# The cross-attention output projection computed with seven block products in place of eight

## The chip, the cores and the metric

The kernel runs on one core of one Trainium2 chip. The metric is the device time of one execution in microseconds (us). Before the change the median of three runs is 860.67 us (860.36 to 862.97).

The engines are called as the profile calls them: PE multiplies matrices (PEld loads its weights beside that), DVE and ACT work on vectors, POOL is used here for small vector operations and for issuing transfers, and SP issues transfers. Each engine carries out its own instructions in order and waits for the others by semaphores.

## The reference

One layer of a hybrid encoder on a sequence of 512 tokens with 1024 features, all in float32:

```
x = x + token_mixer(rmsnorm(x))
x = x + cross_attention(rmsnorm(x), rmsnorm(mem))     # 4 heads of 256, 256 memory tokens
x = x + relu(rmsnorm(x) @ w_up)**2 @ w_down           # 4096 hidden features
y = rmsnorm(x)

def cross_attention(xn, memn):
    q, (k, v) = heads(xn @ w_q), heads(split(memn @ w_kv))
    p = softmax(q @ k.T / 16)
    return concat_heads(p @ v) @ w_o                  # (512 x 1024) @ (1024 x 1024)
```

The change concerns the last line, the product with `w_o`, called `xo` in the kernel.

## The kernel before

**Precision.** Every float32 product is made as three PE products of fp32r parts: each operand is split into hi and lo, and `mm3` (L235 to L238) issues hi by hi, hi by lo and lo by hi. Splitting is `split_out` (L231 to L233): ACT copies the source into hi, DVE subtracts hi from the source into lo.

**Weights.** All weights lie in one packed array of blocks of 128 x 1024 (512 KB). SP streams them in the order of the list `SEQ` into the `st` buffers (three of them), each is split into one of three `wh` and one of three `wl` buffers, and PE takes these in turn. `weights` runs three blocks ahead.

**Cross-attention.** For each head h, `proj_d("xq", ...)` makes the queries, and `xattn_chain(h)` then runs in three pieces: scores and softmax; transposes of the softmax and their split into the buffer `pT` (of the two `as` buffers); the product with the values, whose result for half j of the head is split into a tile of `os_` (128 features by 512 tokens, hi and lo). The chains run inside the projections: `tick` and `drain` emit the next piece. The order on PE in this part is a scheduler's, not written by hand; from the MLP on it is the order of the code.

**The output projection.** `proj_res("xo", 0, os_, ...)` goes over two column halves c. In each, `proj_t` takes four weight blocks q (two 128-feature tiles k each) and four token tiles t: 4 x 4 x 2 matmul triples, 192 matmuls of 128x512 in both halves. The blocks for heads 0 to 2 run first, `drain` finishes head 3, and the fourth block follows. Each finished token tile is added to the residual `xr` (L822, DVE), its squares are summed (`stats`, L816, ACT), and `transp` (L830 on PE, L835 on ACT, L836 on DVE) transposes it into `x3T`, the operand of the MLP.

**The MLP.** It is done for four groups f of 1024 hidden features. `proj_d("up", ...)` makes 128 hidden features at a time; the norm's factor per token, a pow on POOL (L917), is transposed into a row by `rms_row` (L923) after the first block. The down product of a group is a 2 x 2 block product made with seven block products, P1 to P7, instead of eight. Four of them take sums of the blocks of the activations, made by DVE (L1033 to L1036) and split again; four take sums of weight blocks: T2 of three blocks for P6, U of two for P5, T3 of two for P7, and T2 with a fourth block for P4. These sums are made by the DMA: `sum_loads` (L951 in `add_block`) has POOL issue one plain transfer and then accumulating ones into the same place, in two column groups g. T2 and U lie in the two `as` buffers, T3 in two `gate` buffers. Products are gathered in three pairs of PSUM banks, and each is added into the residual or subtracted from it when it ends.

For the first group the sums T2, U and T3 are asked for ahead of the first up projection, behind the cross-attention in the code; they start as soon as their buffers are free.

Of the kernel before, what the change touches and what calls it, by code (L numbers as in the profile page):

```python
# [11 lines left out]
F32R = mybir.dt.float32r  # L12
# [6 lines left out]
P = 128  # L19
# [26 lines left out]
def _split_order():  # L46
    def d(m, c0, n):
        return [("d", m, 0, c0 + P * i) for i in range(n)]

    def t(m, k0, c0, n=4):  # L50
        return [("t", m, k0 + 2 * i, c0) for i in range(n)]

    seq = t("in", 0, 1536) + [("d", "gate", 0, 0)]
    for g in (0, 512, 1024, 2048):
        seq += d("in", g, 2)
    for g in (0, 512, 1024):
        seq += d("in", g + 256, 2)
# [12 lines left out]
    seq += [("t", "down", 8 * f + 2 * g, 512) for f in range(4) for g in range(2)]  # L70
    return seq


SEQ = _split_order()
SIDX = {key: i for i, key in enumerate(SEQ)}
NSTREAM = len(SEQ) - 8


@with_exitstack
def trunk(ctx: ExitStack, tc: tile.TileContext, x, mem, wpk, vec, cst, lmask, rmask, rows, out):  # L80
# [165 lines left out]
            o.append((t[:, b:b + n], t[:, b + n:b + 2 * n]))  # L246
        return o

    def proj_d(mat, c0, xs, n=512, count=2):

        for j in range(count):
            wh, wl = weights(("d", mat, 0, c0 + P * j))
            ps = mmb()
            for k in range(8):
                z = slice(k * P, k * P + P)
                mm3(ps[:, :n], wh[:, z], wl[:, z], xs[k][0], xs[k][1], k == 0, k == 7)
                if k == 3:
                    tick()
            yield ps
            tick()  # L260
# [540 lines left out]
    xr = {}  # L801
# [98 lines left out]
            split_out(d[:, 0:512], d[:, 512:1024], ps)  # L900
            os_[2 * h + j] = hl(d)

    for h in range(4):
        qd[h] = []
        for ps in proj_d("xq", 256 * h, x2):
            d = YT1()
            split_out(d[:, 0:512], d[:, 512:1024], ps)
            qd[h].append(d)
        chains.append(xattn_chain(h))

    st2 = misc[:, 34:42]
    x3T = XT()
    proj_res("xo", 0, os_, (x3T, V_MLP), st2, drain)
    x3 = xk(x3T)
    ms2 = rstd_tok(st2)
    r4 = tiny(4)
    gp.tensor_tensor(out=r4, in0=ms2, in1=nh.to_broadcast([P, 4]), op=ALU.pow)  # L917
    rrow = RG()

    def rms_row():  # L920
        ps = smb()
        for t in range(4):
            pe.transpose(ps[:, t * P:t * P + P], r4[:, t:t + 1].to_broadcast([P, P]), ident)  # L923
        sc.activation(rrow[:, 0:512], ps, AF.Copy)

    ORDER = ("P1", "P2", "P6", "P5", "P7", "P3", "P4")
    JOBS = [("P1", 0), ("P2", 0), ("P1", 1), ("P2", 1)] + [(p, g) for p in ORDER[2:] for g in range(2)]  # L930
    jobs_hl, sums = {}, {}

    def block(f, g, kh, c):
        return SIDX["t", "down", 8 * f + 2 * g + 4 * kh, 512 * c]

    def sum_loads(f, names):

        parts = {"T2": ((0, 1), (1, 1), (0, 0)), "U": ((0, 1), (0, 0)), "T3": ((0, 1), (1, 1))}
        for nme in names:
            t = A16() if nme != "T3" else None  # L940
            for g in range(2):
                sums[f, nme, g] = G4()[:, :] if t is None else t[:, g * 1024:g * 1024 + 1024]
# [12 lines left out]

    def job(f, n):

        if n >= len(JOBS):
            if f < 3:
                split(SIDX["d", "up", 0, 1024 * (f + 1)] + n - len(JOBS))  # L960
            return None
        p, g = JOBS[n]
        if p in PLAIN:
            i = block(f, g, *PLAIN[p])
            split(i)
# [1 line left out]
        if (f, n) not in jobs_hl:  # L967
# [4 lines left out]
            if p == "P6":  # L972
                add_block(s_, block(f, g, 1, 0))
        return jobs_hl[f, n]

    def finish(t, r, first):

# [10 lines left out]
    def add_to(t, c, ps, sign, fin=False):  # L988
# [13 lines left out]
        gp.tensor_tensor(out=r, in0=s1, in1=nh, op=ALU.pow)  # L1002
        finish(t, r, pieces[t])

    ctx.enter_context(tc.manual_schedule(engines={mybir.EngineType.PE}))
    for f in range(4):

# [2 lines left out]
        for p in range(4):  # L1010
            a = []
            for j in range(2):
                ps, = proj_d("up", 1024 * f + P * (p + 4 * j), x3, count=1)
                if f == 0 and p == 0 and j == 0:
                    rms_row()
                y = T2()[:, 0:512]
                v.scalar_tensor_tensor(out=y, in0=ps, scalar=0.0, in1=rrow[:, 0:512], op0=ALU.max, op1=ALU.mult)  # L1017
                sc.activation(y, y, AF.Square)
                a.append(y)
# [10 lines left out]
            sa, sb_ = T2()[:, 0:512], T2()[:, 0:512]  # L1030
            s1, s2, s3, s4 = sa[:, 0:256], sa[:, 256:512], sb_[:, 0:256], sb_[:, 256:512]
            x1, x2_, x3_, x4 = a[0][:, 0:256], a[0][:, 256:512], a[1][:, 0:256], a[1][:, 256:512]
            v.tensor_tensor(out=s1, in0=x2_, in1=x4, op=ALU.subtract)  # L1033
            v.tensor_tensor(out=s2, in0=s1, in1=x1, op=ALU.subtract)  # L1034
            v.tensor_tensor(out=s3, in0=x1, in1=x2_, op=ALU.subtract)
            v.tensor_tensor(out=s4, in0=x3_, in1=s2, op=ALU.add)  # L1036
            ya, yb = YT1(), YT1()
            split_out(ya[:, 0:512], ya[:, 512:1024], sa)
            split_out(yb[:, 0:512], yb[:, 512:1024], sb_)
            e["P5"], e["P6"] = [(ya[:, u:u + 256], ya[:, 512 + u:768 + u]) for u in (0, 256)]  # L1040
            e["P7"], e["P3"] = [(yb[:, u:u + 256], yb[:, 512 + u:768 + u]) for u in (0, 256)]
# [5 lines left out]
        X, Y, Z = [smb(), smb()], [mmb(), mmb()], [smb(), smb()]  # L1047
        bank = {"P1": X, "P2": Y, "P5": Z, "P6": X, "P3": Z, "P7": X, "P4": X}
        into = {"P1": (0, 0, 1), "P2": (0, 0, 1), "P5": (2, 1, 1), "P6": (0, 1, -1), "P3": (0, 1, 1), "P7": (2, 1, -1), "P4": (2, 0, 1)}
        last = {"P2", "P3", "P7", "P4"}  # L1050

        def product(p, g, u, w, first, end):
            for k in range(2):
                ah, al = [t[:, u * P:u * P + P] for t in sta[2 * g + k][p]]
                bh, bl = [t[:, k * 512:k * 512 + 512] for t in w]
                new = first and k == 0 and p in ("P1", "P2", "P5")
                fl = dict(skip_group_check=True)
                ps = bank[p][u]
                pe.matmul(ps, lhsT=ah, rhs=bh, start=new, stop=False, **fl)  # L1059
                pe.matmul(ps, lhsT=ah, rhs=bl, start=False, stop=False, **fl)  # L1060
                pe.matmul(ps, lhsT=al, rhs=bh, start=False, stop=end and k == 1, **fl)  # L1061

        def ahead(n):
            with tc.high_priority():
                for m in range(n, n + 3):
                    job(f, m)
                i = max(hl_tiles)
                for m in range(i + 1, i + 4):
                    load(m)
            if n == 8 and f < 3:  # L1070
                sum_loads(f + 1, ("U", "T3"))
            return job(f, n)

        def done(p, u):
            t0, c, sign = into[p]
            add_to(t0 + u, c, bank[p][u], sign, fin and p in last)

        n = 0
        while n < len(JOBS):
            p, g = JOBS[n]  # L1080
            if p == "P4":
                ws = [ahead(n), ahead(n + 1)]
                for u in range(2):
                    for g in range(2):
                        product(p, g, u, ws[g], False, g == 1)
                    done(p, u)
                n += 2
                continue
            w = ahead(n)
            for u in range(2):  # L1090
                product(p, g, u, w, g == 0, g == 1)
                if g == 1:
                    done(p, u)
            n += 1


# [88 lines left out]
```

## Time and profile before

| | |
|---|---|
| median of the runs | 860.67 us |
| the profiled execution | 861.91 us |
| its span, from the first instruction to the last | 860.1 us |
| mean granted clock of PE | 0.995 |
| matmul instructions of PE in the trace | 4438 |
| weight blocks loaded by SP | 133 of 512 KB, 3.3 us to landing in the median |
| weight blocks loaded by POOL into `as` | 48 of 512 KB, 7.2 us |
| weight blocks loaded by POOL into `gate` | 16 of 512 KB, 7.1 us |

In rows of the profile, `mm<-wh,yT` stands for the output and the operands by the names of the tiles, and `[3.01 <-PE mm L238]` for the idle time ahead of an instruction and what ended it. In this stage `yT` are the head outputs and `x3T` appears as `xT`. The output projection stands at 467.7 to 521 us of the span, with the last pieces of head 3 in it, and the first up projection follows.

### The profile page before, as it was taken

Reading aid. Unit: us, or ns where it says so; the run is one execution under the profiler, and the core shown is the slowest. Engines: PE = TensorE matmul, PEld = TensorE weight load, DVE = VectorE, ACT = ScalarE, POOL = GpSimd, SP = SyncE. Lnnn points to the kernel's source line nnn. Section 1 sums busy time; section 2 is a strip of 40 time slices with the busy share of each in tenths; the row PEclk is TensorE's granted clock in tenths of the full one; section 3 lists DMA queues with packets and bytes.
Section 4 is the critical chain, followed back from the end, with each engine's and each line's share of the span. In section 5 each row is a group of like instructions: output and inputs, shape, how many; then the busy total and the mean of one; then the engine's idle time right before and its main releaser. Section 6 shows DMA issues by size and latency. Waiting matters only on the chain.

```text
span 860.1 us, 11677 instructions
## 1 busy us (share of the span) xinstructions
PE 840.4 (98%) x4438; PEld 693.8 (81%) x4438; DVE 566.6 (66%) x996; ACT 423.7 (49%) x773; POOL 67.4 (8%) x114
## 2 busy tenths in 40 slices
PE   7999999998999999999999999999999999999995
PEld 5888788887987987888888887888888888888884
DVE  5558874599347987654545446676667656856675
ACT  5336454445558576454443346553454344434544
POOL 1000000100010000100001200003101210220001
PEclk9999999999999999999999999999999999999998
DMA  7332223122152232452213852348935993698322
GB/s 265 123 119 75 73 80 136 46 94 76 50 147 74 99 123 99 158 135 98 74 50 110 206 149 76 97 130 229 282 118 127 275 259 99 173 284 203 123 50 98
DMA packets 32682, 113.62 MB, mean 132 GB/s; under 512 B 3761, under 2 KB 3889, under 8 KB 32626
## 3 DMA queue, kind: packets, MB, share of 16 engines
q1 hardware_dynamic: 23120, 78.84, 26.9%
q0 software_dynamic: 9216, 33.56, 17.7%
q8 instruction: 35, 0.57, 0.3%
q10 hardware_dynamic: 290, 0.47, 0.2%
q14 instruction: 21, 0.17, 0.1%
HBM read 110.76 MB, written 2.10 MB: 131 GB/s over the span
## 4 chain that ended last, share of the span: by engine, by line
PE 85%; issue 6%; DVE 5%; DMA 1%; ACT 1%; POOL 1%; POOLq 0%; ACTq 0%; DVEq 0%
PE mm L236 19%; PE mm L237 19%; PE mm L238 18%; PE sm L1059 5%; PE sm L1060 5%; PE sm L1061 5%; PE sm L688 2%; PE sm L673 2%; PE sm L454 2%; DVE wl L233 1%; PE sm L384 1%; PE mm L1060 1%; PE mm L1061 1%; PE mm L1059 1%; DVE a L479 1%
## 5 line engine op out<-in xcount | busy, mean ns | idle before, releaser
L232 ACT ACTIVATE wh<-st 128x1024 fp32r<-128x1024 f32 x133 | 141.1, 1061 | 223.2 <-PE mm L237 118.8
L233 DVE TENSOR_TENSOR wl<-st,wh 128x1024 fp32r<-128x1024 f32 x133 | 162.7, 1223 | 106.8 <-ACT wh L232 101.7
L236 PE MATMUL mm<-xT,wh 128*128 128x512 f32 x544 | 216.0, 398 | 0.0
L237 PE MATMUL mm<-xT,wh 128*128 128x512 f32 x544 | 213.2, 392 | 0.4 <-DVE xT L836 0.4
L238 PE MATMUL mm<-xT,wl 128*128 128x512 f32 x544 | 212.3, 390 | 0.0
L237 PEld LDWEIGHTS mm<-xT,wh 128*128 128x128 f32 x544 | 102.2, 188 | 22.9 <-DVE xT L836 2.0
L236 PEld LDWEIGHTS mm<-xT,wh 128*128 128x128 f32 x544 | 102.2, 188 | 22.2 <-issue 0.7
L238 PEld LDWEIGHTS mm<-xT,wl 128*128 128x128 f32 x544 | 102.1, 188 | 21.3 <-issue 0.2
L951 POOL DMA_DIRECT2D as<-in_wpk x48 | 36.5, 770 | 312.0 <-DVE wl L233 187.2
L1017 DVE SCALAR_TENSOR_TENSOR t<-mm,rg 128x512 f32<-128x512 f32 x32 | 22.1, 691 | 55.1 <-PE mm L238 55.0
L236 PE MATMUL mm<-wh,yT 128*128 128x512 f32 x128 | 50.6, 395 | 0.0
L238 PE MATMUL mm<-wh,yT 128*128 128x512 f32 x128 | 50.4, 394 | 0.0
L237 PE MATMUL mm<-wl,yT 128*128 128x512 f32 x128 | 50.4, 393 | 0.0
L1059 PE MATMUL sm<-wh,yT 128*128 128x512 f32 x128 | 49.8, 389 | 0.0
L1060 PE MATMUL sm<-wl,yT 128*128 128x512 f32 x128 | 49.8, 389 | 0.0
L1061 PE MATMUL sm<-wh,yT 128*128 128x512 f32 x128 | 49.8, 389 | 0.0
L232 ACT ACTIVATE wh<-as 128x1024 fp32r<-128x1024 f32 x24 | 25.5, 1062 | 33.3 <-PE sm L1061 23.7
L233 DVE TENSOR_TENSOR wl<-as,wh 128x1024 fp32r<-128x1024 f32 x24 | 29.4, 1226 | 13.7 <-ACT wh L232 13.7
L174 POOL TENSOR_TENSOR tiny<-tiny,misc 128x4 f32<-128x4 f32 (+1 forms) x14 | 11.9, 850 | 282.5 <-DVE tiny L172 282.5
L990 DVE TENSOR_TENSOR vv<-vv,sm 128x512 f32<-128x512 f32 x48 | 31.0, 680 | 1.2 <-PE sm L1061 1.2
L236 PEld LDWEIGHTS mm<-wh,yT 128*128 128x128 f32 x128 | 24.1, 188 | 5.3 <-DVE a L233 0.5
L232 ACT ACTIVATE yT<-t 128x512 fp32r<-128x512 f32 x32 | 19.8, 630 | 17.0 <-DVE t L1034 16.5
(275 smaller groups left out, 1510.5 us busy)
## 6 DMA issues: line engine op xcount, KB each, us to landing
st<-in_wpk SPq DMA_DIRECT2D x133, 512.0 KB, 3.3
as<-in_wpk POOLq DMA_DIRECT2D x48, 512.0 KB, 7.2
gate<-in_wpk POOLq DMA_DIRECT2D x16, 512.0 KB, 7.1
as<-in_x SPq DMA_DIRECT2D x4, 512.0 KB, 6.3
vv<-in_x SPq DMA_DIRECT2D x8, 256.0 KB, 4.2
out<-vv SPq DMA_DIRECT2D x7, 256.0 KB, 2.3
a<-in_mem SPq DMA_DIRECT2D x2, 512.0 KB, 5.1
t<-in_rows SPq DMA_DIRECT2D x2, 256.0 KB, 6.1
```

What stands on the lines that cost most here:

```text
L232: sc.activation(dst_hi, src, AF.Copy)
L233: v.tensor_tensor(out=dst_lo, in0=src, in1=dst_hi.bitcast(F32), op=ALU.subtract)
L236: pe.matmul(ps, lhsT=ah, rhs=bh, start=first, stop=False)
L237: pe.matmul(ps, lhsT=ah, rhs=bl, start=False, stop=False)
L238: pe.matmul(ps, lhsT=al, rhs=bh, start=False, stop=last)
L454: pe.matmul(ps[:, t * P:t * P + P], lhsT=A[j][:, s * 512 + t * P:s * 512 + t * P + P], rhs=vh[s][:, h * P:h * P + P], start=(s == 0), stop ...
L951: gp.dma_start(out=dst, in_=wpk[idx], **kw)
L990: v.tensor_tensor(out=z, in0=z, in1=ps, op=ALU.add if sign > 0 else ALU.subtract)
L1017: v.scalar_tensor_tensor(out=y, in0=ps, scalar=0.0, in1=rrow[:, 0:512], op0=ALU.max, op1=ALU.mult)
L1059: pe.matmul(ps, lhsT=ah, rhs=bh, start=new, stop=False, **fl)
L1060: pe.matmul(ps, lhsT=ah, rhs=bl, start=False, stop=False, **fl)
L1061: pe.matmul(ps, lhsT=al, rhs=bh, start=False, stop=end and k == 1, **fl)
```

## The change

The projection `xo` is made by the same seven block products as the MLP's down product; the code of the products moves into a function `by_blocks`, which the MLP calls for f = 0 to 3 and the projection with f = -1.

- The 2 x 2 blocks: heads 0 and 1 against heads 2 and 3, the first 256 tokens against the last, and the two column halves of `w_o`.
- ACT copies the unsplit outputs of heads 0 and 1 into `of`. When an output of head 2 or 3 is ready, `forms` makes the four combinations with the output of head 0 or 1 on DVE and splits them. One of the split results of head 3 is put into a part of `x3T` that is free until the products end.
- The weight sums for f = -1 come by 14 accumulating or plain transfers of POOL and two more for P4: T2 and T3 are asked for ahead of head 3's queries, U when head 3 is drained, that is ahead of P6. SP streams the six plain blocks instead of eight.
- The order of products for f = -1 is P1, P2, P6, P7, P5, P3, P4, each for g = 0 and 1.
- Each product is added to the residual as it ends; a tile that is complete goes through `stats` and `transp` as before.
- The first up projection's first blocks (f = 0, p = 0) take features 4 to 7 ahead of 0 to 3 (`LASTK`).

The diff, without the part of the products that only moved (`product`, `ahead` and the loop over the products, which are the same but for what is shown):

```diff
-    seq += t("xo", 0, 0) + t("xo", 0, 512)
+    seq += t("xo", 0, 0) + t("xo", 4, 512, 2)
...
+    seq += t("xo", 0, 512, 2)
...
-NSTREAM = len(SEQ) - 8
+NSTREAM = len(SEQ) - 10
...
-    def proj_d(mat, c0, xs, n=512, count=2):
+    def proj_d(mat, c0, xs, n=512, count=2, ks=range(8)):
...
             os_[2 * h + j] = hl(d)
 
+            if h < 2:
+                if j == 0:
+                    of[h] = A4()
+                sc.activation(of[h][:, j * 512:j * 512 + 512], ps, AF.Copy)
+                continue
+            p = 2 * (h - 2) + j
+            o = of[h - 2][:, j * 512:j * 512 + 512]
+            ya = A4(F32R)[:, :] if h == 2 else x3T[1][:, j * 1024:j * 1024 + 1024]
+            yb = A4(F32R)[:, :]
+            forms(o[:, 0:256], o[:, 256:512], ps[:, 0:256], ps[:, 256:512], ya, yb, sta_o[p])
+            for u, nme in enumerate(("P2", "P4")):
+                sta_o[p][nme] = (d[:, u * 256:u * 256 + 256], d[:, 512 + u * 256:768 + u * 256])
...
+    def forms(x1, x2, x3, x4, ya, yb, e):
+        sa, sb_ = T2()[:, 0:512], T2()[:, 0:512]
+        s1, s2, s3, s4 = sa[:, 0:256], sa[:, 256:512], sb_[:, 0:256], sb_[:, 256:512]
+        v.tensor_tensor(out=s1, in0=x2, in1=x4, op=ALU.subtract)
+        v.tensor_tensor(out=s2, in0=s1, in1=x1, op=ALU.subtract)
+        v.tensor_tensor(out=s3, in0=x1, in1=x2, op=ALU.subtract)
+        v.tensor_tensor(out=s4, in0=x3, in1=s2, op=ALU.add)
+        split_out(ya[:, 0:512], ya[:, 512:1024], sa)
+        split_out(yb[:, 0:512], yb[:, 512:1024], sb_)
...
+    JOBS[-1] = [(p, g) for p in ("P1", "P2", "P6", "P7", "P5", "P3", "P4") for g in range(2)]
...
+        return SIDX["t", "down" if f >= 0 else "xo", max(f, 0) * 8 + 2 * g + 4 * kh, 512 * c]
...
+    LAST = {f: {"P2", "P3", "P4", "P7" if f >= 0 else "P5"} for f in JOBS}
+
+    def by_blocks(f, sta, banks, done, ready=None):
...
+            if ready is not None:
+                ready(p, g)
...
     for h in range(4):
+        if h == 3:
+            sum_loads(-1, ("T2", "T3"))
         qd[h] = []
...
     x3T = XT()
-    proj_res("xo", 0, os_, (x3T, V_MLP), st2, drain)
+
+    def heads_in(p, g):
+
+        while p == "P2" and len(sta_o[2 * g + 1]) < 7:
+            tick()
+        if (p, g) == ("P6", 0):
+            drain()
+            sum_loads(-1, ("U",))
+
+    def add_out(t, c, ps, sign, last):
+        z = xr[t, c]
+        v.tensor_tensor(out=z, in0=z, in1=ps, op=ALU.add if sign > 0 else ALU.subtract)
+        if last:
+            stats(st2, t, c)
+            transp((x3T, V_MLP), t, c)
+
+    for p in range(4):
+        sta_o[p]["P1"] = tuple(t[:, 0:256] for t in os_[p])
+    by_blocks(-1, sta_o, (mm2, mm2, sm2), add_out, heads_in)
+    drain()
...
+    LASTK = (4, 5, 6, 7, 0, 1, 2, 3)
...
-                ps, = proj_d("up", 1024 * f + P * (p + 4 * j), x3, count=1)
+                ps, = proj_d("up", 1024 * f + P * (p + 4 * j), x3, count=1, ks=LASTK if f == p == 0 else range(8))
```

How the change moves instructions, at three places. In the rows a tile's name carries the number of its buffer's use, L-numbers are those of the kernel the rows are of, and `[waits ...]` are the queues or engines whose semaphores an instruction waits for.

**POOL, from head 3's softmax to the pow of the MLP's norm.** Before, the six transfers for the MLP's T2 (`as_4664`) and four for its U (`as_4665`) stand ahead of the pow:

```order
L951 DMA as_4664<-in_wpk 128x1024 [waits DMASW5_49]
L951 DMA as_4665<-in_wpk 128x1024 [waits DMAHW7_49,DVE_49,PE_49]
L951 DMA as_4665<-in_wpk 128x1024 [waits DMASW1_49]
L951 DMA as_4664<-in_wpk 128x1024 [waits DMASW6_49]
L951 DMA as_4665<-in_wpk 128x1024 [waits DMASW3_49,DMASW0_49]
L951 DMA as_4665<-in_wpk 128x1024 [waits DMASW1_49]
L951 DMA as_4664<-in_wpk 128x1024 [waits DMASW7_49]
L917 TENSOR_TENSOR tiny_4659<-tiny_4657,misc 128x4 [waits DVE_49,Pool_49]
```

After, the projection's last two additions to T2 (`as_4055`) and its U (`as_4456`) stand there; the MLP's T3 (`gate_4742`, `gate_4743`), T2 (`as_4740`, six transfers) and U (`as_4741`, four) follow, and the pow is behind them:

```order
L963 DMA as_4055<-in_wpk 128x1024 [waits DMASW0_49,DVE_49]
L963 DMA as_4055<-in_wpk 128x1024 [waits DMASW3_49,DMASW1_49,DVE_49]
L963 DMA as_4456<-in_wpk 128x1024 [waits DMAHW7_49,DVE_49,PE_49]
L963 DMA as_4456<-in_wpk 128x1024
L963 DMA as_4456<-in_wpk 128x1024 [waits DMASW4_49]
L963 DMA as_4456<-in_wpk 128x1024 [waits DMASW5_49]
L963 DMA gate_4742<-in_wpk 128x1024 [waits DVE_49]
L963 DMA gate_4743<-in_wpk 128x1024 [waits DVE_49]
...
L963 DMA as_4741<-in_wpk 128x1024 [waits DMASW3_49]
L1083 TENSOR_TENSOR tiny_4735<-tiny_4733,misc 128x4 [waits DVE_49,Pool_49]
```

What moved: the buffer that held head 3's softmax is now filled with the projection's U, at the place where the MLP's U was loaded.

**DVE, behind head 3's values** (`yT` there). Before, two splits of the values, two weight splits, and the residual adds (`vv`):

```order
L233 TENSOR_TENSOR yT_4318<-sm_4311,yT_4318 128x512
L233 TENSOR_TENSOR yT_4328<-sm_4321,yT_4328 128x512
L233 TENSOR_TENSOR wl_4344<-st_4297,wh_4343 128x1024
L233 TENSOR_TENSOR wl_4374<-st_4347,wh_4373 128x1024
L822 TENSOR_TENSOR vv_3266<-mm_4199,vv_3266 128x512
```

After, the second half of head 3's combinations (`t_716`, `t_717`), with the splits of T3 (`wl_4462`, `wl_4478` from `gate`) among them, then the split of U (`wl_4496` from `as_4456`):

```order
L923 TENSOR_TENSOR t_716_4391<-a_643_4027,sm_4380 128x256
L234 TENSOR_TENSOR a_710_4369<-t_712_4371,a_710_4369 128x512
L924 TENSOR_TENSOR t_716_4391<-t_716_4391,a_643_4027 128x256
L234 TENSOR_TENSOR wl_4462<-gate_4056,wh_4461 128x1024
L234 TENSOR_TENSOR wl_4478<-gate_4057,wh_4477 128x1024
L925 TENSOR_TENSOR t_717_4392<-a_643_4027 128x256
L926 TENSOR_TENSOR t_717_4392<-sm_4380,t_716_4391 128x256
L234 TENSOR_TENSOR xT_4241<-t_716_4391,xT_4241 128x512
L1071 TENSOR_TENSOR vv_3266<-vv_3266,mm_4346 128x512
L234 TENSOR_TENSOR a_715_4390<-t_717_4392,a_715_4390 128x512
L1071 TENSOR_TENSOR vv_3268<-vv_3268,mm_4347 128x512
L234 TENSOR_TENSOR wl_4496<-as_4456,wh_4495 128x1024
```

What moved: between head 3's values and the first residual adds stand the combinations and three weight splits.

**PE, from P6 to P7.** Before, the projection ran on here with the plain weight blocks from `st` and no other operands:

```order
L236 MATMUL mm_4202<-wh_4293,yT_4328 128x512
L237 MATMUL mm_4202<-wl_4294,yT_4328 128x512
L830 MATMUL sm_4432<-cs,vv_3270 128x128 x4
L238 MATMUL mm_4202<-wh_4293,yT_4328 128x512
L236 MATMUL mm_4467<-wh_4343,yT_3873 128x512
L237 MATMUL mm_4467<-wl_4344,yT_3873 128x512
```

After, the end of P6 (`wh_4407`, T2), the transposes of two finished tiles, the first half of P5 (`wh_4495`, U), and P7 (`wh_4461`, T3):

```order
L1005 MATMUL mm_4243<-wh_4407,xT_4241 128x512
L831 MATMUL sm_4421<-cs,vv_3266 128x128 x4
L831 MATMUL sm_4443<-cs,vv_3268 128x128 x4
L1003 MATMUL sm_4529<-wh_4495,a_671_4191 128x512
L1003 MATMUL sm_4530<-wh_4495,a_671_4191 128x512
L1004 MATMUL sm_4529<-wl_4496,a_671_4191 128x512
L1005 MATMUL sm_4529<-wh_4495,a_671_4191 128x512
L1003 MATMUL sm_4529<-wh_4495,a_677_4213 128x512
L1004 MATMUL sm_4529<-wl_4496,a_677_4213 128x512
L1005 MATMUL sm_4529<-wh_4495,a_677_4213 128x512
L1003 MATMUL mm_4242<-wh_4461,a_672_4192 128x512
```

What moved: the scheduler set a half of P5 ahead of P7, although the list of products has P7 first.

More of the change, by code (lines that the diff above doesn't have):

```diff
@@ L901, in xattn_chain @@
             os_[2 * h + j] = hl(d)
[L903 to L912, printed above, removed]
-    proj_res("xo", 0, os_, (x3T, V_MLP), st2, drain)
[L914 to L917, printed above, removed]
@@ L939, in sum_loads @@
         for nme in names:
-            t = A16() if nme != "T3" else None
+            if nme == "T3":
+                t2 = [G4()[:, :] for _ in range(2)]
+            else:
+                t = A16()
+                t2 = [t[:, g * 1024:g * 1024 + 1024] for g in range(2)]
             for g in range(2):
-                sums[f, nme, g] = G4()[:, :] if t is None else t[:, g * 1024:g * 1024 + 1024]
+                sums[f, nme, g] = t2[g]
         for i in range(3):
@@ L974, in job, with product, ahead, finished @@
         return jobs_hl[f, n]
+    INTO = {"P1": (0, 0, 1), "P2": (0, 0, 1), "P5": (2, 1, 1), "P6": (0, 1, -1), "P3": (0, 1, 1), "P7": (2, 1, -1), "P4": (2, 0, 1)}
+    LAST = {f: {"P2", "P3", "P4", "P7" if f >= 0 else "P5"} for f in JOBS}
+    def by_blocks(f, sta, banks, done, ready=None):
+        user = {"P1": 0, "P2": 1, "P5": 2, "P6": 0, "P3": 2, "P7": 0, "P4": 0}
+        held = {}
+        def product(p, g, u, w, first, end):
+            for k in range(2):
+                ah, al = [t[:, u * P:u * P + P] for t in sta[2 * g + k][p]]
+                bh, bl = [t[:, k * 512:k * 512 + 512] for t in w]
+                new = first and k == 0 and p in ("P1", "P2", "P5")
+                fl = dict(skip_group_check=True)
+                ps = held[user[p]][u]
+                pe.matmul(ps, lhsT=ah, rhs=bh, start=new, stop=False, **fl)
+                pe.matmul(ps, lhsT=ah, rhs=bl, start=False, stop=False, **fl)
+                pe.matmul(ps, lhsT=al, rhs=bh, start=False, stop=end and k == 1, **fl)
+        def ahead(n):
+            with tc.high_priority():
+                for m in range(n, n + 3):
+                    job(f, m)
+                i = max(hl_tiles)
+                for m in range(i + 1, i + 4):
+                    load(m)
+            if n == 8 and 0 <= f < 3:
+                sum_loads(f + 1, ("U", "T3"))
+            return job(f, n)
+        def finished(p, u):
+            t0, c, sign = INTO[p]
+            done(t0 + u, c, held[user[p]][u], sign, p in LAST[f])
+        n = 0
+        while n < len(JOBS[f]):
+            p, g = JOBS[f][n]
+            if ready is not None:
+                ready(p, g)
+            if user[p] not in held:
+                held[user[p]] = banks[user[p]]()
+            if p == "P4":
+                ws = [ahead(n), ahead(n + 1)]
+                for u in range(2):
+                    for g in range(2):
+                        product(p, g, u, ws[g], False, g == 1)
+                    finished(p, u)
+                n += 2
+                continue
+            w = ahead(n)
+            for u in range(2):
+                product(p, g, u, w, g == 0, g == 1)
+                if g == 1:
+                    finished(p, u)
+                elif ready is not None:
+                    tick()
+            n += 1
@@ new lines, in add_out @@
+    def add_out(t, c, ps, sign, last):
[8 more added lines that the diff above has]
+    drain()
+    x3 = xk(x3T)
+    ms2 = rstd_tok(st2)
+    r4 = tiny(4)
+    gp.tensor_tensor(out=r4, in0=ms2, in1=nh.to_broadcast([P, 4]), op=ALU.pow)
@@ L1046, in trunk @@
             nc.sync.dma_start(out=gfin, in_=rows[3:4, :].to_broadcast([P, D]))
[L1047 to L1094, printed above, removed]
+        by_blocks(f, sta, (sm2, mm2, sm2), lambda t, c, ps, sign, last: add_to(t, c, ps, sign, fin and last))
 def _consts():
```

56 lines of the change are left out of this document (30 added, 26 removed).

## The prediction

> **What bounds the kernel now.** I read the page's busy table and the chain of work that ended last first.
>
> ```profile
> span 860.1 us, 11677 instructions
> PE 840.4 (98%) x4438; PEld 693.8 (81%) x4438; DVE 566.6 (66%) x996; ACT 423.7 (49%) x773; POOL 67.4 (8%) x114
> PE 85%; issue 6%; DVE 5%; DMA 1%; ACT 1%; POOL 1%; POOLq 0%; ACTq 0%; DVEq 0%
> ```
>
> PE is busy 98% of the span and carries 85% of the chain, so a matmul removed is time saved, as long as nothing else ends later. An average over the span can't settle that: the table of stretches for the projection does.
>
> ```profile
> 467.70:482.60 14.90, 14.90 (x82) 12.82 (x81) 8.01 (x16) 6.56 (x14) 1.74 (x2) 1.00 0.77 198
> 482.60:493.90 11.30, 11.30 (x52) 9.17 (x51) 3.98 (x6) 2.85 (x4) 4.61 (x6) 1.00 0.88 211
> 493.90:500.00 6.10, 6.10 (x36) 5.09 (x36) 4.47 (x11) 5.71 (x18) 0.00 (x0) 1.00 1.05 262
> 500.00:521.20 21.20, 21.20 (x101) 17.50 (x100) 9.54 (x21) 8.76 (x23) 0.00 (x0) 1.00 0.35 110
> 521.20:528.60 7.40, 7.24 (x35) 4.87 (x33) 5.59 (x16) 5.55 (x16) 1.03 (x1) 1.00 0.22 74
> ```
>
> After the stretch and its length come the busy times of PE, PEld, DVE, ACT and POOL. PE has no gap worth naming before 521.2 us. DVE (3.98 of 11.30 us) and ACT (2.85) have room there, and the DMA engines are full from 482.6 to 500 us (0.88 and 1.05). The one wait of PE between 475 and 535 us is this:
>
> ```profile
> PE mm L237 <- DVE xT L836: 0.2, 1, 0.2
> ```
>
> So the projection is the work of PE alone now, and there is no wait in it that the change could take away. What it can give is the matmuls; what it can cost is new waits.
>
> **What a matmul is worth.** From the timeline of PE:
>
> ```profile
> 470.43 0.28 PE L236 MATMUL sm<-a,yT 128*128 128x256 f32 x1
> ...
> 473.30 0.40 PE L236 MATMUL mm<-wh,yT 128*128 128x512 f32 x1
> ...
> 476.05 1.09 PE L887 MATMUL sm<-cs,t 128*128 128x128 f32 x8
> 476.90 0.48 PE L236 MATMUL mm<-wh,yT 128*128 128x512 f32 x1
> ...
> 482.23 0.39 PE L238 MATMUL sm<-as,a 128*128 128x512 f32 x1
> 482.45 0.39 PE L236 MATMUL mm<-wh,yT 128*128 128x512 f32 x1
> ...
> 485.85 0.39 PE L236 MATMUL mm<-wh,yT 128*128 128x512 f32 x1
> ...
> 520.62 0.60 PE L830 MATMUL sm<-cs,vv 128*128 128x128 f32 x4
> 520.97 0.47 PE L238 MATMUL mm<-wh,yT 128*128 128x512 f32 x1
> ...
> 528.57 0.47 PE L236 MATMUL mm<-xT,wh 128*128 128x512 f32 x1
> ```
>
> From 482.45 to 485.85 stand 15 matmuls: 0.2267 us each, start to start. Four transposes take 0.35 us (520.62 to 520.97), the 24 score matmuls 2.87, the eight transposes of the softmax 0.85. I compare one stretch, from head 3's scores (470.43) to the first up matmul with j = 1 (528.57): 58.14 us. Ahead of it and behind it PE has the same instructions in both kernels. It holds 180 matmuls of the projection, 12 of head 3's values and 24 of the first up block (216 x 0.2267 = 48.97), scores 2.87, softmax 0.85, nine groups of four transposes 3.15: 55.84 us. The other 2.3 us are slack, nearly all behind 521 us.
>
> **The saving.** 192 matmuls become 7 x 2 x 2 x 2 x 3 = 168: 24 x 0.2267 = **-5.44 us**, and the work of the stretch is 50.40 us.
>
> **New wait 1: DVE makes the combined operands of head 3.** The times of its instructions, back to back, stand in DVE's timeline in the MLP, where the same four additions and splits run; three groups of the projection's stretch follow (after the bar: busy time and mean ns).
>
> ```profile
> 546.07 1.23 DVE L233 TENSOR_TENSOR wl<-st,wh 128x1024 fp32r<-128x1024 f32 x1 [0.18 <-ACT wh L232]
> 547.22 0.42 DVE L1033 TENSOR_TENSOR t<-t,t 128x256 f32<-128x256 f32 x1
> 547.55 0.68 DVE L233 TENSOR_TENSOR a<-t,a 128x512 fp32r<-128x512 f32 x1
> 548.15 0.42 DVE L1034 TENSOR_TENSOR t<-t,t 128x256 f32<-128x256 f32 x1
> ```
>
> ```profile
> L232 ACT ACTIVATE wh<-st 128x1024 fp32r<-128x1024 f32 x10 | 10.6, 1060 | 19.3 <-PE mm L238 16.3 <-PE mm L237 2.9
> L835 ACT ACTIVATE xT<-sm,vc 128x128 fp32r<-128x128 f32 x32 | 10.1, 362 | 1.8 <-DVE xT L836 1.7
> L836 DVE SCALAR_TENSOR_TENSOR xT<-sm,vc,xT 128x128 fp32r<-128x128 f32 x32 | 9.7, 345 | 3.0 <-ACT xT L835 2.6
> ```
>
> A weight split holds DVE 1.14 us, an addition of 256 columns 0.34, a pass over 512 columns 0.60. Before, head 3's values end at 482.45. Now a weight split for P6 stands ahead of the split of the softmax on ACT and on DVE (1.06 + 1.23), and its buffer comes free only when P2 has used it; I put the end of the values at 485.1, with other matmuls filling PE. From 484.6 DVE has one split (0.69), eight additions (2.72), seven passes over 512 columns (4.20: five splits, two adds into the residual) and two weight splits of T3 that stand among them (2.28): 9.9 us, done at 494.5. PE has until then 26 matmuls and eight transposes, 6.6 us, up to 491.7; the last group waits for the second add and ends at 494.9. That is **3.3 us** of wait. The chain of heads 0 to 2 is made earlier, beside matmuls that don't need it: nothing.
>
> **New wait 2: U.** P5's weight sum U takes the buffer in which head 3's softmax stands, so its first transfer waits for the last matmul of head 3's values. In before the same transfers, for the MLP, wait for the same matmul, so POOL's timeline shows how they run; the DMA view has the landings of those issued at 482.92 (the first), 469.37 (accumulating), 486.62 and 489.27 (both accumulating).
>
> ```profile
> 482.92 2.02 POOL L951 DMA_DIRECT2D as<-in_wpk  x3 [11.40 <-PE sm L238]
> 486.62 0.86 POOL L951 DMA_DIRECT2D as<-in_wpk  x1 [1.67 <-DMA as<-in_wpk]
> 489.27 1.73 POOL L951 DMA_DIRECT2D as<-in_wpk  x2 [1.79 <-DMA as<-in_wpk]
> 525.92 1.03 POOL L917 TENSOR_TENSOR tiny<-tiny,misc 128x4 f32<-128x4 f32 x1 [34.93 <-DVE tiny L842]
> ```
>
> ```profile
> as<-in_wpk POOLq DMA_DIRECT2D x1, 512.0 KB, 3.4
> as<-in_wpk POOLq DMA_DIRECT2D x1, 512.0 KB, 7.3
> as<-in_wpk POOLq DMA_DIRECT2D x1, 512.0 KB, 9.0
> as<-in_wpk POOLq DMA_DIRECT2D x1, 512.0 KB, 9.6
> ```
>
> A plain transfer of 512 KB lands after 3.4 us, an accumulating one after 7.3 to 9.6. The first block's sum was there 12.7 us after the first issue (486.62 + 9.0 - 482.92). In before that cost nothing: the sum was wanted a whole up projection later. Now P5 stands 38 matmuls and transposes behind. Issue at 485.2, landing at 485.2 + 12.7 = 497.9 (bounds: 3.4 + 7.3 gives 496.1, 5.5 + 9.6 gives 500.3), hi on ACT 1.06, lo on DVE 1.23: 500.2 us. PE, which would be there at 494.9, waits **4.85 us**. I take 497.9 because it is the same pair of transfers beside the same kind of traffic. Together both waits lie between 4.4 (U in time) and 10.6 (U at 500.3). Queued behind these transfers on POOL are only the MLP's, wanted a whole up projection later; behind U's split on DVE stand the two residual adds of P6.
>
> [...]
>
> **Waits after that.** Two adds of P6 stand on DVE behind U's split, and P7 writes the same banks: some 0.3 us. The adds of P7 and P5 between splits (0.60 and 1.14 each), the second U split and the P4 splits give about 1.7 more at three product changes (0.35, 0.85, 0.45): **2.0 us**, between 0 and 4. No row of before shows these; the value is my walk along DVE's order with the times above.
>
> **The transition to the MLP.** In before the last 521.2 to 528.6 us lose some 1.2 us of the slack to evacuation. Now from P3's end to the last residual add, DVE has two adds, one add, three weight splits and ten passes of L836 at about the 0.36 of ACT's L835 that they alternate with: 1.8 + 3.4 + 3.9 = 9.1, the add itself 0.6 and 0.4 for the first matmul to drain: 10.1. PE has 24 matmuls and three groups (6.5), then 12 up matmuls that need only the second column half (2.7): 9.2. Four transposes (0.35) and four pairs of L835/L836 follow before PE runs on. That gives **3.4 us** of waits (between 1.2, as now, and 5). The reordered k loop is what hides the 2.7 us; without it they would be paid too.
>
> **Costed at nothing.** The copies of heads 0 and 1 on ACT (four of about 0.6 us; ACT had 49% of the span), T2 and T3, which are issued before head 3's scores and whose buffers are free long before, and the pow on POOL that makes the MLP norm's factor: it stood at 525.92 and now stands behind the MLP's ten transfers, which wait for this stage's sums to be used. I put it ready at 528 to 532, wanted at 534.5, three to six us of cover.
>
> **The sum.** Waits 0.2 + 3.3 + 4.85 + 2.0 + 3.4 = 13.75 on work of 50.40 is 64.15 us, against 58.14: **+6.0 us**. From the other end: U's split at 500.2, then 118 matmuls (26.75), seven groups (2.45) and 5.4 of waits is 534.6, +6.0 to 528.57. The profiled run took 861.91 us for its span of 860.1, the median of the runs is 860.67, so 867.9 on the profile's scale and **866.7 us** on the median's.
>
> **Rivals.**
> Rival A, *U lands at the plain pace* (no change): both transfers take about 3.5, U is there at 492.5, and P5 is bound by DVE's chain and U's split behind it: 496.1 instead of 500.2, so 4.1 less: about +2, 862.9 us. It decides if an accumulating transfer lands in under 4.5 us. Against it are all four accumulating rows; for it, that SP streams fewer blocks at that time than at 482 to 500 us in before.
> Rival B, *the saving comes through* (faster): PE's waits total 4 us rather than 13.75, because DVE and the transfers run 8 to 10 us ahead of my walk: 50.4 + 4 = 54.4, -3.7, 857 us; with 3 us, 856. The room of DVE in the stretches (3.98 of 11.30) speaks for it, the fixed order behind the head-3 values against.
> Rival C, *worse* (over 869.5): the transfers share with more traffic (both accumulations 9.6 or more), the pow on POOL is late, or the pause slows PE. [...]
>
> **How the numbers follow.** Forecast (864 to 869.5) 0.62, rival A 0.17, rival B 0.12, rival C 0.09. A measurement tells 0.3% (2.6 us) from no change: below 858.1 faster, above 863.25 slower. Rival A lies mostly within, with a little of the forecast's lower edge: same 0.18; rival B faster: 0.12; slower 0.70. The range reaches to rival A and the middle of C, and leaves out B's most and C's worst: 859.5 to 871.
>
> **What would show it.** Step by step, in the profile after: 24 matmuls fewer; a gap of PE ahead of P5, released by the split of U, ending near 500 us, with U's accumulating transfers at 7 us or more; DVE's chain for head 3 ending near 494.5; two or three waits of PE under 1 us at later products; 3.4 us before the up projection; POOL's pow before PE wants it. If PE's gap ahead of P5 is under 2 us or the accumulations land in 4, the forecast is wrong.

## The result and the profile after

The changed kernel takes 868.54 us in the median of six runs (867.80 to 870.25), the kernel before 860.68 in its six. The ratio is 1.0091, with a 95% interval of 1.0075 to 1.0107: slower by 0.9%, or 7.9 us. The forecast was 866.7, in a range of 859.5 to 871. The two profiled executions stand only 6.1 us apart (868.05 and 861.91): in the one of before the granted clock was 0.50 from 212.91 to 216.32 us, far ahead of the change, and in the other it was 1.00 there, so that the changed program is 1.5 us earlier when the stage begins.

The page of the changed kernel, the span, the busy table, the clock in 40 slices and the chain:

```profile
span 866.1 us, 11716 instructions
PE 838.3 (97%) x4414; PEld 688.3 (79%) x4414; DVE 587.1 (68%) x1032; ACT 437.0 (50%) x791; POOL 79.5 (9%) x130
PEclk9999999999999999999999998999999999999998
PE 81%; issue 6%; DVE 6%; DMA 5%; ACT 1%; POOL 1%; POOLq 0%; ACTq 0%; DVEq 0%
```

The 24 matmuls are gone (4438 to 4414), and PE's share of the chain fell from 85% to 81%, with DMA risen from 1% to 5%: PE now waits for something that goes back to transfers. One slice of the clock shows an 8 where before had a 9.

The waits of PE between 462 and 545 us, in total, times, and the longest; before had 0.2 us in one:

```profile
PE sm L1089 <- POOL tiny L1083: 3.8, 1, 3.8
PE mm L1005 <- DVE xT L234: 1.0, 1, 1.0
PE sm L831 <- DVE vv L1071: 0.9, 2, 0.6
PE mm L1003 <- ACT xT L233: 0.9, 1, 0.9
PE mm L238 <- DVE xT L837: 0.7, 1, 0.7
PE mm L237 <- ACT xT L836: 0.6, 1, 0.6
PE sm L1004 <- DVE wl L234: 0.5, 1, 0.5
PE sm L1003 <- ACT wh L233: 0.5, 1, 0.5
```

The longest is none of those that the forecast put a price on. It is the pow of the MLP's norm (L1083), for which the transposes of L1089 wait. PE's timeline has the place of most (the two that end with `xT L837` and `xT L836` stand at 523.18 and 525.30, in the transition to the MLP); in brackets stands the wait that the trace puts ahead of the row:

```profile
489.23 0.50 PE L1003 MATMUL mm<-wh,xT 128*128 128x512 f32 x1 [0.86 <-ACT xT L233]
491.43 0.73 PE L1005 MATMUL mm<-wh,xT 128*128 128x512 f32 x2 [1.00 <-DVE xT L234]
493.31 0.63 PE L831 MATMUL sm<-cs,vv 128*128 128x128 f32 x4 [0.57 <-DVE vv L1071]
494.43 0.73 PE L1003 MATMUL sm<-wh,a 128*128 128x512 f32 x2 [0.48 <-ACT wh L233]
495.69 0.50 PE L1004 MATMUL sm<-wl,a 128*128 128x512 f32 x1 [0.53 <-DVE wl L234]
...
506.74 0.65 PE L831 MATMUL sm<-cs,vv 128*128 128x128 f32 x4 [0.34 <-DVE vv L1071]
...
528.40 0.40 PE L239 MATMUL mm<-xT,wl 128*128 128x512 f32 x1
532.61 1.11 PE L1089 MATMUL sm<-cs,tiny 128*128 128x128 f32 x4 [3.81 <-POOL tiny L1083]
533.38 0.78 PE L237 MATMUL mm<-xT,wh 128*128 128x512 f32 x1
533.95 0.63 PE L238 MATMUL mm<-xT,wh 128*128 128x512 f32 x1
534.38 0.63 PE L239 MATMUL mm<-xT,wl 128*128 128x512 f32 x1
```

Measured from start to start, less what the instruction ahead takes (0.2267 us for a matmul, 0.35 for four transposes), the five places up to 495.69 lose 4.6 us and the pow 3.98 (528.40 to 532.61). After the pow the matmuls stand 0.43 us apart, not 0.227. The table of stretches shows why; the granted clock is the third value from the end:

```profile
526.00:530.00 4.00, 2.80 (x11) 1.45 (x9) 1.31 (x4) 1.84 (x4) 0.89 (x1) 1.00 1.01 377
530.00:534.00 4.00, 1.39 (x6) 1.29 (x7) 0.96 (x1) 0.24 (x1) 1.93 (x2) 0.68 0.98 215
534.00:538.00 4.00, 4.00 (x11) 3.13 (x10) 1.12 (x2) 1.40 (x3) 0.00 (x0) 0.50 0.84 168
538.00:542.00 4.00, 4.00 (x18) 3.23 (x18) 0.57 (x1) 0.80 (x1) 0.00 (x0) 0.97 0.00 0
```

The clock fell to half and came back at about 538 us. Twelve matmuls and four transposes paid 2.7 us for it. Why the pow came so late is in POOL's timeline:

```profile
502.53 1.09 POOL L963 DMA_DIRECT2D as<-in_wpk  x2 [3.06 <-DVE wl L234]
...
518.64 1.95 POOL L963 DMA_DIRECT2D as<-in_wpk  x3 [2.41 <-DMA as<-in_wpk]
528.10 0.89 POOL L963 DMA_DIRECT2D as<-in_wpk  x1 [7.52 <-DMA as<-in_wpk]
530.63 0.87 POOL L963 DMA_DIRECT2D as<-in_wpk  x1 [1.64 <-DMA as<-in_wpk]
531.20 1.36 POOL L1083 TENSOR_TENSOR tiny<-tiny,misc 128x4 f32<-128x4 f32 x1
```

POOL starts the MLP's T2 at 502.53, when the projection's late sum has been split, and issues each accumulating transfer only when the one that it adds to has landed. For the last two it stood waiting 7.52 and 1.64 us (the plain transfers of the MLP's U, to which they add, took 8.6 and 10.6), with the pow behind them. The pow's input was ready at 525.1 us, as DVE's timeline has it:

```profile
524.97 0.17 DVE L843 TENSOR_SCALAR tiny<-tiny 128x4 f32<-128x4 f32 x1
```

### The profile page after: what moved, and what is told of

It reads as the page before. It is cut to its first block, busy times and chain, and to the rows that moved or that the text cites. A ratio compares the mean times of both kernels' runs of the same rounds, so it can differ in the third digit from the quotient of the medians.

```text
span 866.1 us, 11716 instructions
## 1 busy us (share of the span) xinstructions
PE 838.3 (97%) x4414; PEld 688.3 (79%) x4414; DVE 587.1 (68%) x1032; ACT 437.0 (50%) x791; POOL 79.5 (9%) x130
## 4 chain that ended last, share of the span: by engine, by line
PE 81%; issue 6%; DVE 6%; DMA 5%; ACT 1%; POOL 1%; POOLq 0%; ACTq 0%; DVEq 0%
PE mm L237 17%; PE mm L238 17%; PE mm L239 16%; PE sm L1004 5%; PE sm L1003 5%; PE sm L1005 5%; DMA as<-in_wpk 3%; PE sm L689 2%; PE sm L674 2%; PE sm L455 2%; DVE wl L234 2%; PE mm L1003 1%; PE sm L385 1%; PE mm L1004 1%; PE mm L1005 1%
## 5 line engine op out<-in xcount | busy, mean ns | idle before, releaser
L233 ACT ACTIVATE wh<-st 128x1024 fp32r<-128x1024 f32 x131 | 139.0, 1061 | 207.6 <-PE mm L238 116.1
L234 DVE TENSOR_TENSOR wl<-st,wh 128x1024 fp32r<-128x1024 f32 x131 | 160.3, 1224 | 87.6 <-ACT wh L233 82.6
L963 POOL DMA_DIRECT2D as<-in_wpk x60 | 45.7, 777 | 336.3 <-DVE wl L234 192.5
L233 ACT ACTIVATE wh<-as 128x1024 fp32r<-128x1024 f32 x30 | 31.8, 1061 | 38.2 <-PE sm L1005 25.3
L234 DVE TENSOR_TENSOR wl<-as,wh 128x1024 fp32r<-128x1024 f32 x30 | 36.8, 1226 | 18.1 <-ACT wh L233 18.1
L1004 PE MATMUL sm<-wl,a 128*128 128x512 f32 x76 | 29.8, 392 | 0.5 <-DVE wl L234 0.5
L1003 PE MATMUL sm<-wh,a 128*128 128x512 f32 x76 | 29.6, 392 | 0.5 <-ACT wh L233 0.5
L1005 PE MATMUL sm<-wh,a 128*128 128x512 f32 x76 | 29.6, 389 | 0.0
L1005 PEld LDWEIGHTS sm<-wh,yT 128*128 128x128 f32 x128 | 24.0, 188 | 5.0
```

Of the source, the lines that this page charges most:

```text
L233: sc.activation(dst_hi, src, AF.Copy)
L234: v.tensor_tensor(out=dst_lo, in0=src, in1=dst_hi.bitcast(F32), op=ALU.subtract)
L963: gp.dma_start(out=dst, in_=wpk[idx], **kw)
```

## The experiments

All ratios are to runs of the kernel before on the same chip, whose median there was 861.8 to 862.1 us. The changed kernel stands at 1.0091.

**The pow ahead of the transfers.** One line ahead of the pow, from which POOL keeps the order of the code:

```diff
+    ctx.enter_context(tc.manual_schedule(engines={mybir.EngineType.Pool}))
     gp.tensor_tensor(out=r4, in0=ms2, in1=nh.to_broadcast([P, 4]), op=ALU.pow)
```

> The changed kernel with one line more: from the pow of the MLP's norm on, POOL keeps the order of the code, so that the pow stands ahead of the fourteen transfers of the MLP's T3, T2 and U instead of behind them. PE, DVE, ACT and SP have the same order as in the changed kernel. Theory (queue): in the profile of the changed kernel PE waits 3.98 us for the pow and then runs 12 matmuls and four transposes at a spacing of 0.43 instead of 0.227 us (2.7 us), and the pow's input had been ready 6.1 us before it ran. Both go: 868.5 - 6.7 = 861.8 us (861 to 863). Rival (late anyway): the statistics of the last tile are what is late, and the wait is only renamed; then 866 us or more. A second rival: the MLP's sums, which now start some 20 us later, come too late for P6 of the first group; then the gain is given back there, as a PE wait at about 574 us, and the time stays at 866 or above.

Measured: ratio 1.0012 (1.0000 to 1.0023), 862.59 us in the median of 12 runs. That is 0.8% less than the changed kernel, 6.8 us for 6.7 expected. The pow now runs when its input is there, and no wait for the MLP's sums follows:

```profile
528.54 1.03 POOL L1084 TENSOR_TENSOR tiny<-tiny,misc 128x4 f32<-128x4 f32 x1 [36.91 <-DVE tiny L843]
```

The other seven lines of PE's waits read the same as in the changed kernel (1.0, 0.9, 0.9, 0.7, 0.6, 0.5 and 0.5 us), so only the wait for the pow went. So the queue theory holds and both rivals fall. The 12 runs spread from 860.75 to 864.85; the last section comes back to that.

**U early, T3 late.** The two sums change places, and P5 goes ahead of P7:

```diff
-    JOBS[-1] = [(p, g) for p in ("P1", "P2", "P6", "P7", "P5", "P3", "P4") for g in range(2)]
+    JOBS[-1] = [(p, g) for p in ("P1", "P2", "P6", "P5", "P7", "P3", "P4") for g in range(2)]
...
-            if nme == "T3":
+            if nme == ("T3" if f >= 0 else "U"):
...
-    LAST = {f: {"P2", "P3", "P4", "P7" if f >= 0 else "P5"} for f in JOBS}
+    LAST = {f: {"P2", "P3", "P4", "P7"} for f in JOBS}
...
-            sum_loads(-1, ("T2", "T3"))
+            sum_loads(-1, ("T2", "U"))
...
-            sum_loads(-1, ("U",))
+            sum_loads(-1, ("T3",))
```

> The changed kernel with the projection's U in the two gate buffers, which are free early, and its T3 in the late buffer instead, and with P5 ahead of P7 in the list of products (as in the MLP). The pow stays where it was. Theory: U's wait goes (PE waited 0.77 and 0.81 us for its split), and as T3's splits no longer stand among head 3's combinations on DVE (2.3 us), so do most of the waits for these (1.02, 1.17, 0.85). That is 4 us ahead of P7, but the pow, which is bound by POOL's queue, gives part of it back: 865 to 867.5 us. If the gain of 4 us is kept whole (POOL's queue moves with PE): 864.5. Rival (my prediction as it was written, in which U alone costs 4.85 us and the combinations 3.3): up to 8 us less, 860.5.

Measured: ratio 1.0058 (1.0043 to 1.0072), some 2.8 us less than the changed kernel (865.7 on the scale of 868.5): inside the theory's numbers, and not the rival's 8 us. In its profile the pow still costs a wait (3.16 us at 531.61), as expected. The waits for the late sum ahead of P5 can't be read there, because the granted clock was 0.50 from 492.48 to 495.89 us.

**Both edits.**

> Both edits: the pow ahead of the MLP's transfers, and U early with T3 late. If the two costs are separate, 868.5 - 6.7 - 4 = 857.8 us (856.5 to 859.5), which is faster than the kernel before (860.7). If one hides the other (T3 late in place of U, or the MLP's sums late), 860 or more.

Measured: ratio 0.9987 (0.9978 to 0.9995), 859.6 us on the scale of 860.7. The second edit gave 2.2 us on top of the first, not 4. PE's two waits for U's split are gone, as expected. The miss is in the profile's timeline of DVE:

```profile
489.08 0.42 DVE L924 TENSOR_TENSOR t<-t,a 128x256 f32<-128x256 f32 x1
489.52 2.36 DVE L234 TENSOR_TENSOR wl<-gate,wh 128x1024 fp32r<-128x1024 f32 x2
491.80 0.42 DVE L925 TENSOR_TENSOR t<-a 128x256 f32<-128x256 f32 x1
```

I had expected the two weight splits to leave the chain of head 3's combinations with T3. They stand there still; they are only U's now. Whichever sum is ready early is split there, and PE's waits of 0.85, 1.00 and 0.57 us ahead of P5 stayed.

**The first group's products ahead of head 3.**

```diff
+    JOBS[-1][2:8] = [("P2", 0), ("P6", 0), ("P5", 0), ("P2", 1), ("P6", 1), ("P5", 1)]
...
-        if (p, g) == ("P6", 0):
+        if (p, g) == ("P2", 1):
             drain()
```

> As the last, and the products in the order P1 (both groups), P2 g0, P6 g0, P5 g0, then P2 g1, P6 g1, P5 g1, P7, P3, P4: twelve matmuls that don't need head 3 (2.7 us) stand ahead of those that do, and are cover for head 3's combinations. Theory: whatever PE still waits for these in the last kernel goes, 0.5 to 2 us less than it: 856 to 858 us. Rival: T3, which is late now, is wanted at the same time as before, and P7 waits for it; then the same as the last kernel.

Measured: ratio 0.9971 (0.9961 to 0.9980), 1.4 us less than the last, inside the 0.5 to 2 of the theory. On the scale of 860.7 that is 858.2 us; the theory's 856 to 858 counted from the 857.8 that the last kernel had not reached. The waits for the combinations are gone, and the rival came true in part. One wait was left:

```profile
500.16 0.47 PE L1004 MATMUL mm<-wh,a 128*128 128x512 f32 x1 [2.17 <-DVE vv L1072]
```

P7 writes where P6 was read, and the residual add of P6 that it waits for stood on DVE behind the split of T3 (in order of time it is the first of P6's two adds; the other ran at 503.71):

```profile
497.93 1.23 DVE L234 TENSOR_TENSOR wl<-as,wh 128x1024 fp32r<-128x1024 f32 x1 [2.94 <-ACT wh L233]
499.07 0.34 DVE L837 SCALAR_TENSOR_TENSOR xT<-sm,vc,xT 128x128 fp32r<-128x128 f32 x1
499.33 0.68 DVE L1072 TENSOR_TENSOR vv<-vv,mm 128x512 f32<-128x512 f32 x1
```

DVE was idle for 2.94 us with that add in its queue. After it the clock was 0.63 for 4 us.

**T3 early too.** Head 3's softmax goes into a half of the MLP's operand tile that is free then, so the late buffer is free after head 2:

```diff
-        pT = T("as", 2560, 2, F32R)
+        pT = T("as", 2560, 2, F32R) if h < 3 else x3T[1][:, 2048:4096]
...
+        if (p, g) == ("P2", 0):
+            sum_loads(-1, ("T3",))
         if (p, g) == ("P2", 1):
             drain()
-            sum_loads(-1, ("T3",))
```

> As the last kernel (the pow first, U early, the products of the first group ahead of head 3), and head 3's softmax stands in a free half of the MLP's operand tile instead of in the late buffer, so that T3's transfers start when head 2 is done, some 17 us earlier. In the last kernel PE waited 2.17 us ahead of P7: the second residual add of P6 stood on DVE behind the split of T3, whose last transfer landed at 496.8 us, and the granted clock fell to 0.63 in the 4 us after it (about 1.6 us more). Theory: both go, and the 24 matmuls saved show at last: ratio to before 0.993 (856 us where before is 861.9). Rival: something else is late in its place (the second residual add, or the last tiles' transposes), and less than 1.5 us is gained: 0.9955 or more.

Measured: ratio 0.9928 (0.9915 to 0.9942), 854.63 us, as expected. It beats both kernels, the one before by 6.2 us. In the waits between 462 and 545 us PE has one left, and the matmuls that the change removed show in full (the lines are in the next section):

```profile
PE mm L238 <- DVE xT L837: 0.4, 1, 0.4
```

The granted clock is 1.00 in every stretch from 486 to 542 us.

**The pow last again, in the best kernel.** Only POOL's order differs:

```diff
-    ctx.enter_context(tc.manual_schedule(engines={mybir.EngineType.Pool}))
```

> The best kernel so far (ratio 0.9928), and only the pow goes back behind the MLP's fourteen transfers on POOL; the order of PE, DVE, ACT and SP stays. Theory (queue): the pow's place is bound by when the projection gives its buffers back, not by PE. In the changed kernel the first transfer of the MLP's T2 started at 502.5 us, when the late sum had been split, and the pow ran 28.7 us later. In the best kernel that split ends at 496.4 us, so the pow would run at 525.2 and end at 526.4, while its input is ready at 519.3 and PE wants it at 521.7: a wait of 4.7 us, and with a fall of the clock 2 us more. Ratio 0.998 to 1.001 (860 to 862.7 us where before is 861.8): with the pow last, the seven products are worth nothing even without any other wait. Rival: with the stage shorter the transfers have less beside them and run faster, and the pow is in time: ratio 0.994 or less.

Measured: ratio 1.0023 (1.0012 to 1.0034), 8 us more than the best kernel, and somewhat over the theory's 1.001. The pow ran at 527.12 (525.2 expected): the 29.3 us after the first transfer of T2 that the changed kernel had shown as 28.7, only that this transfer started at 497.8. So the rival falls: the transfers ran no faster. PE waited 5.53 us for the 4.7 expected:

```profile
528.53 1.11 PE L1091 MATMUL sm<-cs,tiny 128*128 128x128 f32 x4 [5.53 <-POOL tiny L1085]
```

One instruction at the end of a queue takes away all that the seven products give.

**The k order of the first up projection,** alone in the kernel before, and taken out of the kernel with the pow first (`ks=range(8)` for all).

> The kernel before with nothing changed but the order of k in the first up projection (features 4 to 7 first). In before the second column half is the late one, so the reordered loop asks first for what comes last: PE waits for the last tile's transposes and evacuation with 12 matmuls (2.7 us) less of cover, ratio 1.003 (1.002 to 1.004). Rival: the order of k is worth something by itself, ratio 1.000 or below.

Measured: ratio 1.0036 (1.0022 to 1.0050). In its profile PE waits 0.78 us for a last residual add (at 523.48) and 1.67 us for the evacuation behind it (at 525.81), where the kernel before waits 0.16.

> The kernel with the pow first (ratio 1.0012), without the reordered k loop in the first up projection: features 0 to 3 first, as before the change. Prediction's step: the reordered loop hides 2.7 us of the last tile's evacuation behind 12 matmuls, so without it PE waits that much longer: ratio 1.004 (865 us). Rival: PE's wait only moves within the block, since all 24 matmuls need the last tile before they end: no more than 0.5 us, ratio 1.0018 or less.

Measured: ratio 1.0059 (1.0044 to 1.0074), 4 us more than with the reordered loop; 2.7 were expected. The one wait that it makes is in PE's timeline, and the clock after it (0.67) in the table of stretches:

```profile
528.10 0.66 PE L831 MATMUL sm<-cs,vv 128*128 128x128 f32 x4 [3.83 <-DVE vv L1071]
```

```profile
530.00:534.00 4.00, 4.00 (x14) 3.19 (x14) 1.05 (x3) 0.85 (x3) 3.59 (x7) 0.67 0.61 212
```

So the loop's order is worth nothing by itself. It gains 4 us where the first column half is the late one, as in the changed kernel, and costs 3 where the second is, as in before.

## Why the prediction came true, and where it did not

The time came out inside the range, in good part by luck: U and the waits behind it were priced 4.75 us too high, and the pow with the fall of the clock, put at nothing, cost 6.7.

- **The saving** (-5.44 us): right. Before the change six more matmuls of the projection stand ahead of head 3's scores than after it, so the forecast's stretch doesn't hold the same work in both; a longer one does, from head 0's first row maximum to the second up block's first DVE step. These are its ends before and in the best kernel, where PE has one wait of 0.4 us:

```profile
419.63 0.69 DVE L870 TENSOR_REDUCE tiny<-sm 128x2 f32<-128x512 f32 x1 [1.41 <-PE sm L238]
534.32 0.69 DVE L1017 SCALAR_TENSOR_TENSOR t<-mm,rg 128x512 f32<-128x512 f32 x1 [1.59 <-PE mm L238]
```

```profile
418.36 0.69 DVE L871 TENSOR_REDUCE tiny<-sm 128x2 f32<-128x512 f32 x1 [1.41 <-PE sm L239]
527.82 0.69 DVE L1138 SCALAR_TENSOR_TENSOR t<-mm,rg 128x512 f32<-128x512 f32 x1 [1.60 <-PE mm L239]
```

  That is 114.69 us before and 109.46 there: -5.2. The other 1.0 of the 6.2 us lies outside this stretch, and its cause is not shown; the 1.3 us between the two starts go with the fall of the clock at 212.91 us that only the profile of before has.
- **New wait 1, head 3's combinations:** right. DVE's chain was put at 9.9 us, up to 494.5; it ran from 483.22 to 493.17, 9.95 us, in a program that stands 1.5 us earlier at that point (418.13 against 419.63 at the same instruction). The waits are 3.0 us (1.02, 1.17 and 0.85), for 3.3.
- **New wait 2, U:** the first wrong step. It was put at 497.9, with a wait of 4.85 us behind the combinations. The first transfer was issued at 483.99 and the accumulating one landed at 493.3, 9.3 us in all and not 12.7; PE waited 1.6 us for it (0.77 and 0.81). That is under the 2 us that the prediction itself named as the sign of being wrong. The accumulating transfer itself took 5.4 us:

```profile
as<-in_wpk POOLq DMA_DIRECT2D x1, 512.0 KB, 5.4
```

  Why it was faster is shown in part only. The 9.0 us row of before had another accumulating transfer under way when it was issued (483.99 to 491.97), and behind T2's last addition, which landed at 486.05, this one had none. But nor had the 7.3 us row, and each of the two had a plain one under way at its issue and the next accumulating one 1.3 to 1.4 us behind it; what makes 7.3 of the one and 5.4 of the other stays open. Rival A's point was 4.5 us; on this step it was nearer than the forecast.
- **Waits after that** (2.0): 0.5 us, at 506.74. **The transition** (3.4): 2.9 us, by the places of PE between 522 and 528 us.
- **Costed at nothing, the pow:** the second wrong step, and the dearer one. The forecast had it ready at 528 to 532 and wanted at 534.5. It ended at 532.56, which is 534.1 on the forecast's clock (1.5 us later): two us past its latest, and even so in time for 534.5. But PE wanted it at 528.6, 530.1 on that clock, because the waits ahead were shorter, most of all that for U. So what they gave back went straight into the wait for the pow, 3.98 us, and the clock took 2.7 on top. The experiments show this step both ways: with the pow ahead of the transfers 6.8 us go, and with it put back behind them in the best kernel 8 come.

Waits of 13.75 us were forecast; 4.6 + 0.5 + 2.9 + 3.98 + 2.7 = 14.7 were measured. Some 1.9 us more are in pieces of under 0.3 us, mostly at changes between matmuls and transposes, for which the sum has no term. In all the longer stretch takes 123.3 us in the changed kernel (418.13 to 541.43), 8.6 more than before, where the forecast had 6.0 more. Rival C's mechanism (the pow late, the clock down) made 6.7 us of it, more than any other: A was nearer about U, and C was right about the end.

The prediction has slips that change little: ten passes at 0.36 us are 3.6 and not 3.9, the sum from the other end is 534.8 and not 534.6, 500.2 less 494.9 is 5.3 and not 4.85, and the accumulating rows that it shows against rival A are three, not four. Its rows are also not the whole spread: in before the plain transfer issued at 483.46 took 5.5 us, and the accumulating one issued at 489.81 took 12.9.

## What to carry to other kernels

Where a tuned stage has no wait of its bound engine, a cheaper algorithm brings its matmuls only if nothing new ends later: list each queue on which a short instruction stands behind waiting transfers, since here a 1 us pow behind fourteen of them cost more than 24 matmuls gave, and moving it was one line. A margin between two forecast times is no cover, because an earlier wait that is priced too high hides the later one. And a sum that an engine waits for belongs in a buffer that comes free early, for its split blocks the evacuations behind it too (here the residual add of P6 behind the split of T3, and PE waited 2.17 us).

## What the runs showed of the hardware

**The transfers of 512 KB named here took 3.6 to 10.6 us.** All are of the changed kernel. Two accumulating ones that overlapped for 2.2 us (issued at 477.72 and 480.74) took 5.2 and 5.3, and U's second group and the MLP's T2, with more beside them, 6.5 to 8.5. A plain one took 3.6 (issued at 483.99) and, as the third of three issued within 1.1 us, 10.6 (at 519.72).

**The falls of the clock named here came behind 3.41 us in which PE was busy for 0.81 to 1.85, with one wait or several.** The falls from 1.00 to 0.50 lasted 3.41 us in the profile of before (from 212.91), with the pow first (from 497.87) and with U early (from 492.48), and 6.82 in that of the changed kernel (from 531.40). In the 3.41 us ahead of the fall PE was busy for 1.08 us in before and for 0.81 in the changed kernel, and for 1.24 ahead of that at 501.05 with the first group's products ahead (one wait of 2.17 us). With the pow first the fall stands behind five waits that none reached 1.2 us each:

```profile
494.45:497.87 3.42, 1.85 (x8) 1.16 (x9) 2.17 (x4) 2.86 (x8) 0.00 (x0) 1.00 0.71 139
497.87:501.28 3.41, 3.41 (x10) 2.63 (x9) 2.80 (x9) 1.80 (x6) 0.00 (x0) 0.50 0.02 5
```

With U early, the wait of 3.3 us for the pow (528.28 to 531.61) lies in these two stretches, and the clock stays up:

```profile
526.61:530.02 3.41, 1.84 (x8) 0.90 (x6) 1.25 (x3) 1.42 (x2) 1.28 (x2) 1.00 1.04 316
530.02:533.44 3.42, 1.83 (x10) 1.62 (x11) 1.11 (x2) 0.60 (x1) 1.53 (x2) 1.00 1.03 201
```

The five short waits left the clock at 1.00 in the changed kernel's profile, with PE busy for 1.85 us from 490.44 to 493.85 and for 2.41 from 493.85 to 497.27. So the same 1.85 us stood ahead of a fall in one profile and not in the other; what decides between them is not shown. The 12 runs with the pow first differ in the clock too: their mean granted clock is 0.994 to 0.996 in the six up to 862.1 us and 0.992 in the five from 864.3 on.
